# Moving the gate's blocks among key, value and query blocks, and the band values beside the heads' outputs, in a one-core encoder block

## The chip, the core and the metric

The kernel runs on one core of a Trainium2 chip. A core has five engines that run side by side, each in its own order: TensorE (PE, the matrix multiplier, with PEld its weight loads), VectorE (DVE), ScalarE (ACT), GpSimd (POOL) and SyncE (SP, which issues the DMAs here). Data lies in DRAM, in SBUF (128 partitions) and, for matmul results, in PSUM (eight banks of 128 partitions x 512 float32 values). The metric is the time of one execution in microseconds (us); lower is better.

## What is computed

One layer of an encoder on 512 tokens of width 1024: two token mixers on one normalised input, merged by gates, then cross-attention and a feed-forward part.

```python
h = rmsnorm(x, norm_mix[l])
qa, ka, va, za, alpha, beta, qb, kb, vb, ga, gb = _split_cols(h @ w_in[l], IN_SPLITS)
qkv = jax.nn.silu(_causal_dwconv(jnp.concatenate([qa, ka, va], axis=-1), conv_w[l]))
qa, ka, va = _split_cols(qkv, (A_QK, A_QK, A_VW))
oa = _gated_deltanet(qa, ka, va, alpha, beta, a_log[l], dt_bias[l])     # mixer A, 8 heads of 128
oa = rmsnorm(oa, head_norm[l]) * jax.nn.silu(za.reshape(b, s, A_HEADS, A_DV))
ob = _chunk_band_attention(qb, kb, vb, band_bias)                       # mixer B, 16 heads of 64
y = jax.nn.sigmoid(ga) * (oa @ w_a_out[l]) + jax.nn.sigmoid(gb) * (ob @ w_b_out[l])
x = x + y @ w_o[l]
x = x + _memory_xattn(rmsnorm(x, norm_xattn[l]), rmsnorm(mem, norm_mem[l]), ...)
x = x + (jax.nn.silu(gate) * up) @ w_down[l]
```

The gated delta rule of mixer A needs, for each head and each pair of chunks, the inverse of a unit lower triangular matrix I + L, where L comes from the keys' products k k^T. The value blocks, the gates and the band values depend on h alone.

## The kernel before

**Split matmuls.** Each weight tile is loaded (`raw`), copied to a reduced float form on ScalarE (`whi`, L114), and the rest, `raw - whi`, is formed as `wlo` (L116) on VectorE or GpSimd, whichever `lo_eng` names. The input h has a high and a low part too (`hh`, `hl`). A product is three matmuls: hi x hi, hi x lo, lo x hi (L140 to L142). A block (`block_steps`) is a projection to 128 features for all 512 tokens: eight steps of three matmuls of 512 columns. A natural group (`natural`, L165 to L167) has the tokens on the partitions: per 128 tokens eight steps of three matmuls of 256 columns. Tiles of raw, whi and wlo have three buffers each, of 128 x 1024 values.

**The stretch with keys and values.** Key blocks `k0` to `k7` (`ka` in PSUM) are followed by value blocks `v0` to `v7` (`va`), query blocks (`qa`) and, among them, groups `z1` to `z3` of mixer A's output gate za. A block's second part is put on a pending list and goes on one step at a time while later blocks issue their matmuls: for a key the causal convolution (`conv`, a ScalarE and three VectorE passes, L349 and L351), then `kT` (L355), twelve steps later four matmuls `kk` of the key with itself (L388), and the decay terms that give L (L412, L416 to L418; GpSimd's `PT` L401). For a value it is the convolution, `vT`, and twelve steps later four transposes `vn` (L499) and `vs` (L502).

**The inverse.** The diagonal 32 x 32 blocks of all L go to DRAM (`d1`) and come back as one tile `Lg`; `inverse_blocks` inverts them by 31 steps of two VectorE instructions on a growing tile: `sub` (L518) and `X` (L520). A copy (L523) and a way through DRAM (`d2`; writes, GpSimd's memsets L531, eight loads of X and eight of L, L539 and L540) follow, and then `inverse_levels` puts the blocks together on PE (first matmul `t`, L556), in four sets, two for each half of the loads, each a step apart.

**Behind it.** The queries go on, beside `states`, which runs the recurrence over the chunks. Then stands the gate of mixer A, `gate_a` (blocks `ga`, then ScalarE's tanh L655 into `sga`), beside `head_out` for each head: matmuls `oU` (L464) and `oS` (L468), ScalarE and VectorE work on the head's output, and its product with the za part (`zs`, L489). Then come the band values `vb_all` (natural groups, evacuated by ScalarE at L638), beside `oa_tiles`: per head four transposes `oaT` (L794) and the split `oah` (ScalarE) and `oal` (VectorE, L118); then `proj_a`, the projection of mixer A, and mixer B.

**What sets the order.** PE's order is the order in which the code emits its matmuls (`manual_schedule`). `drive` emits a main list of steps (blocks), after each advances what is pending, and adds `rate` steps of a side generator for each main step once `delay` steps have gone. The other engines' orders are set by a scheduler when the program is built; at run time each engine keeps its order and waits where an operand is missing. PSUM tags are `mm` (three buffers, blocks and natural groups), `ms` (two: kk, vn, kq, oU, oS, oaT) and `sd` (three, states and inverse levels).

```python
go("z1 k0 k1 k2 k3 k4 k5")
lo_eng[0] = nc.gpsimd
go("k6 k7")
go("v0 v1 v2 v3 v4 v5 z2 v6 v7 z3 q0 q1 q2", side=inverse_blocks(), rate=0.8, delay=22)
go("q3 q4 q5 q6 q7", side=states(), rate=1.0, delay=0)
lo_eng[0] = nc.vector
drive((gate_a(), None), side=seq(*[head_out(hd) for hd in heads]), rate=1.0, delay=12)
drive((vb_all(), None), side=oa_tiles(), delay=12, rate=0.2)
run_all(proj_a())
```

So `wlo` of k6, k7, all values, z2, z3 and all queries is GpSimd's work.

## Time and profile before

| | us |
|---|---|
| median of three runs | 1258.32 (1258.08 to 1258.97) |
| the profiled execution | 1259.04, its span 1257.3 |
| PE busy | 1222.9 (97%) |
| VectorE busy | 682.7 (54%) |
| ScalarE busy | 528.9 (42%) |
| GpSimd busy | 204.1 (16%) |

The page divides the span into 40 slices; a digit is the busy share in tenths, 9 for 90% or more. PE shows 9 in nearly all slices from the sixth on; VectorE shows 8 and 9 in the third to the sixth and 3 to 6 in most later ones. Starts in the rows are counted from the start of the span, and a row in a timeline gives start, duration, engine, line, operation, output and inputs, and in brackets the idle time before it with what ended it. The duration of a matmul is longer than its distance to the next, since matmuls are pipelined.

### The profile page before, as it was taken

The numbers are of one execution on the slowest core, as the hardware profiler recorded it, in microseconds if no ns is written. First come the engines' busy times: TensorE is split into PE (matmuls) and PEld (weight loads), VectorE is DVE, ScalarE is ACT, GpSimd is POOL, SyncE is SP. The second block draws the span as 40 slices with busy tenths as digits, with TensorE's granted clock in tenths as the row PEclk, the third lists the DMA queues.
The fourth block names the chain that finished last, engine by engine and source line by source line (L and its number), as shares of the span: only waits on it lengthen the run. The fifth ranks groups of instructions, "written<-read, shape, count | busy, mean of one in ns | idle before, by whom it ended". The sixth has DMA issues, their size and how long they took to land.

```text
span 1257.3 us, 17665 instructions
## 1 busy us (share of the span) xinstructions
PE 1222.9 (97%) x6899; PEld 1030.1 (82%) x6899; DVE 682.7 (54%) x1272; ACT 528.9 (42%) x1042; POOL 204.1 (16%) x158
## 2 busy tenths in 40 slices
PE   8998889999999999999999999999999999999997
PEld 7776787988898887777788898888888888888887
DVE  6989983564433378876355565446343443432234
ACT  6534235556442266765423444334332232222232
POOL 4356233201200000000122300003211111110000
PEclk9999989999999999999999999999999999999999
DMA  6253233122223333232334453213323323223343
GB/s 205 69 138 97 68 114 89 36 68 76 83 68 103 98 101 101 77 87 90 101 97 118 129 173 116 64 34 118 98 86 101 94 91 101 86 90 93 106 114 124
DMA packets 54612, 122.67 MB, mean 98 GB/s; under 512 B 16993, under 2 KB 23553, under 8 KB 54529
## 3 DMA queue, kind: packets, MB, share of 16 engines
q1 hardware_dynamic: 53440, 120.50, 31.9%
q8 instruction: 54, 0.88, 0.3%
q10 hardware_dynamic: 1088, 1.05, 0.2%
q14 instruction: 30, 0.24, 0.1%
HBM read 117.85 MB, written 3.69 MB: 97 GB/s over the span
## 4 chain that ended last, share of the span: by engine, by line
PE 84%; DVE 9%; issue 3%; ACT 2%; DMA 2%; POOL 1%; SPq 0%; POOLq 0%; DVEq 0%; ACTq 0%
PE ff L142 7%; PE ff L140 7%; PE ff L141 7%; PE g L140 5%; PE g L142 5%; PE g L141 5%; PE nat L165 2%; PE nat L167 2%; PE nat L166 2%; DVE conv L351 2%; PE pt L758 2%; PE ob L766 2%; PE qa L140 1%; DVE X L520 1%; PE kb L140 1%
## 5 line engine op out<-in xcount | busy, mean ns | idle before, releaser
L114 ACT ACTIVATE whi<-raw 128x1024 fp32r<-128x1024 f32 (+3 forms) x205 | 211.9, 1034 | 428.8 <-PE ff L141 157.7
L116 DVE TENSOR_TENSOR wlo<-raw,whi 128x1024 fp32r<-128x1024 f32 (+2 forms) x183 | 230.2, 1258 | 151.3 <-ACT whi L114 148.4
L140 PE MATMUL ff<-xh,whi 128*128 128x512 f32 x352 | 139.1, 395 | 0.0
L142 PE MATMUL ff<-xh,wlo 128*128 128x512 f32 x352 | 138.9, 395 | 0.0
L141 PE MATMUL ff<-xl,whi 128*128 128x512 f32 x352 | 138.9, 395 | 0.0
L206 POOL TENSOR_TENSOR acc<-acc,sq 128x512 f32<-128x512 f32 (+1 forms) x33 | 47.7, 1446 | 312.3 <-ACT sq L205 180.6
L142 PEld LDWEIGHTS ff<-xh,wlo 128*128 128x128 f32 x352 | 66.3, 188 | 15.5
L141 PEld LDWEIGHTS ff<-xl,whi 128*128 128x128 f32 x352 | 66.3, 188 | 15.5
L140 PEld LDWEIGHTS ff<-xh,whi 128*128 128x128 f32 x352 | 66.3, 188 | 15.3
L1058 POOL TENSOR_TENSOR fa<-fa,rrow 128x512 f32<-128x512 f32 x22 | 38.7, 1758 | 199.3 <-ACT fa L1057 194.1
L116 POOL TENSOR_TENSOR wlo<-raw,whi 128x1024 fp32r<-128x1024 f32 x22 | 53.2, 2420 | 85.9 <-ACT whi L114 76.3
L165 PE MATMUL nat<-whi,hh 128*128 128x256 f32 x192 | 57.7, 301 | 6.9 <-DVE conv L351 6.9
L1061 DVE TENSOR_TENSOR fb<-ff,fa 128x512 f32<-128x512 f32 x22 | 15.2, 692 | 77.1 <-PE ff L142 74.4
L166 PE MATMUL nat<-whi,hl 128*128 128x256 f32 x192 | 56.4, 294 | 0.0
L167 PE MATMUL nat<-wlo,hh 128*128 128x256 f32 x192 | 56.4, 294 | 0.0
L142 PE MATMUL g<-guh,wlo 128*128 128x512 f32 x132 | 51.4, 390 | 0.0
L141 PE MATMUL g<-gul,whi 128*128 128x512 f32 x132 | 51.4, 390 | 0.0
L140 PE MATMUL g<-guh,whi 128*128 128x512 f32 x132 | 51.4, 390 | 0.0
L1056 DVE TENSOR_TENSOR fa<-ff,rrow 128x512 f32<-128x512 f32 x22 | 15.2, 692 | 60.9 <-PE ff L142 59.4
L742 ACT ACTIVATE P<-P,mx 128x128 f32<-128x128 f32 (+1 forms) x64 | 35.8, 560 | 29.6 <-DVE mx L740 29.4
L728 POOL MEMSET bias<- 64x64 f32 x16 | 2.3, 144 | 265.5 <-DMA bias<-in_bias 248.3
L165 PEld LDWEIGHTS nat<-whi,hh 128*128 128x128 f32 x192 | 39.0, 203 | 7.7 <-issue 7.6
(380 smaller groups left out, 3189.0 us busy)
## 6 DMA issues: line engine op xcount, KB each, us to landing
raw<-in_w_g SPq DMA_DIRECT2D x22, 512.0 KB, 3.5
raw<-in_w_u SPq DMA_DIRECT2D x22, 512.0 KB, 3.5
raw<-in_w_d SPq DMA_DIRECT2D x20, 512.0 KB, 3.6
raw<-in_wk SPq DMA_DIRECT2D x8, 512.0 KB, 3.6
raw<-in_wv SPq DMA_DIRECT2D x8, 512.0 KB, 3.7
raw<-in_wq SPq DMA_DIRECT2D x8, 512.0 KB, 3.6
raw<-in_wga SPq DMA_DIRECT2D x8, 512.0 KB, 3.6
bias<-in_bias SPq DMA_DIRECT2D x16, 256.0 KB, 2.8
```

Of the source, the lines that this page charges most:

```text
L114: nc.scalar.activation(hi, src, AF.Copy, scale=1.0 if scale is None else scale)
L116: (eng or nc.vector).tensor_tensor(out=lo, in0=src, in1=hi.bitcast(F32), op=ALU.subtract)
L140: nc.tensor.matmul(out=ps[:, :w], lhsT=hi[:, k - a, :], rhs=xh[:, n], start=first, stop=False)
L141: nc.tensor.matmul(out=ps[:, :w], lhsT=hi[:, k - a, :], rhs=xl[:, n], start=False, stop=False)
L142: nc.tensor.matmul(out=ps[:, :w], lhsT=lo[:, k - a, :], rhs=xh[:, n], start=False, stop=last)
L165: nc.tensor.matmul(out=o, lhsT=xh[:, tok], rhs=hi[:, kw, :], start=(k == 0), stop=False)
L166: nc.tensor.matmul(out=o, lhsT=xl[:, tok], rhs=hi[:, kw, :], start=False, stop=False)
L167: nc.tensor.matmul(out=o, lhsT=xh[:, tok], rhs=lo[:, kw, :], start=False, stop=(k == KD - 1))
L206: nc.gpsimd.tensor_tensor(out=acc, in0=acc, in1=sq, op=ALU.add)
L351: nc.vector.scalar_tensor_tensor(out=c[:, s:], in0=ps[:, : T - s], scalar=w(3 - s), in1=c[:, s:], op0=ALU.mult, op1=ALU.add)
L742: nc.scalar.activation(pr, pr, AF.Exp, scale=-1.0, bias=mx, accum_out=rs[:, t : t + 1])
L1058: nc.gpsimd.tensor_tensor(out=a, in0=a, in1=row3, op=ALU.mult)
```

## The change

**Gate blocks.** The eight blocks of `gate_a` are no longer a phase of their own. They are entries `g0` to `g7` of the lists that `go` works off, between key, value and query blocks; their `wlo` goes to GpSimd. After such a block `gate_after` applies the tanh into a temporary tile and writes it to DRAM (`dga`); `head_out` loads it back into `sga` for its head.

**Low parts.** `lo_eng` now stays on VectorE until q3. So the `wlo` of k6, k7, v0 to v7 and q0 to q2 moves from GpSimd to VectorE; the gate blocks, z2 and z3 (by the new argument `eng`) have theirs on GpSimd, and q3 to q7 as before.

**Band values and transposes.** `vb_all` stands beside the heads' outputs in place of the gate, with rate 1.5 and delay 6 where rate 1.0 and delay 12 stood. It evacuates through a temporary tile to DRAM (`dvb`), from where the eight `vb` tiles are loaded after `proj_a`. The transposes of a head and their split (`oa_tile`) become the last steps of the next head's `head_out`, with `oah` and `oal` in the tags `c` and `b`.

```diff
-    def weights(src, kt, width):
+    def weights(src, kt, width, eng=None):
...
-        split(hi, lo, raw, eng=lo_eng[0])
+        split(hi, lo, raw, eng=eng or lo_eng[0])
...
-    def gemm(store, name, w, hd):
+    def gemm(store, name, w, hd, eng=None):
         store[hd] = PM(name)
-        yield from block_steps(store[hd], w[hd], h)
+        yield from block_steps(store[hd], w[hd], h, eng=eng)
...
+        s = sga[hd] = G("b", "sga")
+        nc.sync.dma_start(out=s, in_=dga[hd])
+        if hd:
+            yield from oa_tile(hd - 1)
+        if hd == AH - 1:
+            yield from wait(6)
+            yield from oa_tile(hd)
+
+    sga, oa = {}, []
+
+    def oa_tile(hd):
+        z = zs[hd // 2]
+        o = (hd % 2) * P
+        pt = PS("oaT")
+        for n in range(NT):
+            nc.tensor.transpose(out=pt[:, n * P : n * P + P], in_=z[:, n, o : o + P], identity=ident)
+        hi, lo = G("c", "oah", F32R), G("b", "oal", F32R)
+        split(hi, lo, pt, gain(C_HN, 0))
+        oa.append((hi, lo))
+        yield
...
     def vb_all():
-        vb.extend([G("b", "vb") for _ in range(2)] for tt in range(NT))
         for g in range(4):
             def ev(tt, ps, g=g):
-                nc.scalar.activation(vb[tt][g // 2][:, (g % 2) * 256 : (g % 2) * 256 + 256], ps[:, 0:256], AF.Copy)
+                v = TMP("vbt", "c")[:, :256]
+                nc.scalar.activation(v, ps[:, 0:256], AF.Copy)
+                nc.sync.dma_start(out=dvb[tt, :, g * 256 : g * 256 + 256], in_=v)
             yield from natural(wvb[g], 256, h, NT, ev)
 
     def z_group(g):
-        yield from natural(wz[g - 1], 256, xg if g <= 1 else h, NT, z_evac(g))
+        yield from natural(wz[g - 1], 256, xg if g <= 1 else h, NT, z_evac(g), nc.gpsimd if g > 1 else None)
...
-    def gate_a():
-        for j in range(KD):
-            ps = PM("ga")
-            yield from block_steps(ps, wga[j], h)
-            s = G("b", "sga")
-            nc.scalar.activation(s, ps, AF.Tanh, scale=0.5)
-            sga.append(s)
-            yield
...
+    def gate_after(j):
+        s = TMP("sga", "th")
+        nc.scalar.activation(s, gaps[j], AF.Tanh, scale=0.5)
+        nc.sync.dma_start(out=dga[j], in_=s)
+        yield
...
+    gh = lambda j: (gemm(gaps, "ga", wga, j, nc.gpsimd), gate_after(j))
...
-    go("z1 k0 k1 k2 k3 k4 k5")
-    lo_eng[0] = nc.gpsimd
-    go("k6 k7")
+    go("z1 k0 k1 k2 k3 g0 k4 k5 g1 k6 k7 g2")
...
-    go("v0 v1 v2 v3 v4 v5 z2 v6 v7 z3 q0 q1 q2", side=inverse_blocks(), rate=0.8, delay=22)
+    go("v0 v1 g3 v2 v3 g4 v4 v5 g5 z2 v6 v7 g6 z3 q0 q1 g7 q2", side=inverse_blocks(), rate=0.8, delay=22)
...
-    drive((gate_a(), None), side=seq(*[head_out(hd) for hd in heads]), rate=1.0, delay=12)
+    drive((vb_all(), None), side=seq(*[head_out(hd) for hd in heads]), rate=1.5, delay=6)
...
-    drive((vb_all(), None), side=oa_tiles(), delay=12, rate=0.2)
     run_all(proj_a())
+    for tt in range(NT):
+        vb.append([G("b", "vb") for _ in range(2)])
+        for x in range(2):
+            nc.sync.dma_start(out=vb[tt][x], in_=dvb[tt, :, x * T : x * T + T])
```

**How instructions move.** The rows below are an engine's instructions in their order, with line, operation, output, inputs and shape; a number at a name's end only tells one tile from another.

PE, where the first inverse-level matmuls `t` stand. Before, v7, z3 and the whole of q0 (`qa_1991`) lie ahead of them, and q1 (`qa_2042`) goes on between the sets:

```order
L140 MATMUL qa_1991<-hh_548,whi_1994 128x512
L141 MATMUL qa_1991<-hl_549,whi_1994 128x512
L142 MATMUL qa_1991<-hh_548,wlo_1995 128x512
L556 MATMUL t_418_2022<-X_380_1767,L 32x32 x16
L140 MATMUL qa_2042<-hh_436,whi_2045 128x512
L141 MATMUL qa_2042<-hl_437,whi_2045 128x512
L142 MATMUL qa_2042<-hh_436,wlo_2046 128x512
L556 MATMUL t_427_2061<-X_380_1767,L 32x32 x16
```

After, v7 (`va_2002`) is the last block ahead of them, and g6 (`ga_2062`) goes on between the sets:

```order
L140 MATMUL va_2002<-hh_550,whi_2005 128x512
L141 MATMUL va_2002<-hl_551,whi_2005 128x512
L142 MATMUL va_2002<-hh_550,wlo_2006 128x512
L576 MATMUL t_419_2042<-X_385_1799,L 32x32 x16
L140 MATMUL ga_2062<-hh_438,whi_2065 128x512
L141 MATMUL ga_2062<-hl_439,whi_2065 128x512
L142 MATMUL ga_2062<-hh_438,wlo_2066 128x512
L576 MATMUL t_428_2081<-X_385_1799,L 32x32 x16
```

So z3 and q0 moved from ahead of the levels to behind them, and g0 to g5 now lie ahead.

VectorE in the inverse, at the same steps (`sub` and `X` of 24 x 8 to 21 x 11). Before, only the passes of `conv` and a `vs` stand between the steps:

```order
L520 TENSOR_TENSOR X_1349<-X_1349,sub_1420 128x24x8
L518 TENSOR_TENSOR sub_1445<-Lg_1347,X_1349 128x207
L520 TENSOR_TENSOR X_1349<-X_1349,sub_1445 128x23x9
L351 SCALAR_TENSOR_TENSOR conv_1499<-va_1423,cst,conv_1499 128x511
L518 TENSOR_TENSOR sub_1451<-Lg_1347,X_1349 128x220
L351 SCALAR_TENSOR_TENSOR conv_1499<-va_1423,cst,conv_1499 128x510
L520 TENSOR_TENSOR X_1349<-X_1349,sub_1451 128x22x10
L351 SCALAR_TENSOR_TENSOR conv_1499<-va_1423,cst,conv_1499 128x509
L502 TENSOR_TENSOR vs_1533<-vn_1528,dinv_970 128x512
```

After, a low part `wlo` stands there too:

```order
L540 TENSOR_TENSOR X_1453<-X_1453,sub_1518 128x24x8
L538 TENSOR_TENSOR sub_1543<-Lg_1451,X_1453 128x207
L540 TENSOR_TENSOR X_1453<-X_1453,sub_1543 128x23x9
L116 TENSOR_TENSOR wlo_1648<-raw_1645,whi_1647 128x1024
L538 TENSOR_TENSOR sub_1549<-Lg_1451,X_1453 128x220
L351 SCALAR_TENSOR_TENSOR conv_1532<-va_1459,cst,conv_1532 128x511
L540 TENSOR_TENSOR X_1453<-X_1453,sub_1549 128x22x10
L351 SCALAR_TENSOR_TENSOR conv_1532<-va_1459,cst,conv_1532 128x510
L538 TENSOR_TENSOR sub_1555<-Lg_1451,X_1453 128x231
L351 SCALAR_TENSOR_TENSOR conv_1532<-va_1459,cst,conv_1532 128x509
L540 TENSOR_TENSOR X_1453<-X_1453,sub_1555 128x21x11
```

So a weight's low part, GpSimd's before, moved in between two steps, with its convolution passes after it.

GpSimd from the memsets of X, just ahead of the inverse. Before, low parts of values, of z2 and z3 and of q0 follow (two tiles for a z group):

```order
L512 MEMSET X_1349 128x1024
L513 MEMSET X_1349 128x32
L116 TENSOR_TENSOR wlo_1492<-raw_1489,whi_1491 128x1024
L116 TENSOR_TENSOR wlo_1556<-raw_1553,whi_1555 128x1024
L116 TENSOR_TENSOR wlo_1562<-raw_1559,whi_1561 128x1024
L116 TENSOR_TENSOR wlo_1747<-raw_1744,whi_1746 128x1024
L116 TENSOR_TENSOR wlo_1784<-raw_1781,whi_1783 128x1024
L116 TENSOR_TENSOR wlo_1839<-raw_1836,whi_1838 128x1024
L116 TENSOR_TENSOR wlo_1845<-raw_1842,whi_1844 128x1024
L116 TENSOR_TENSOR wlo_1995<-raw_1992,whi_1994 128x1024
```

After, the low parts of g4, g5 and z2 (two) are left ahead of the memsets for the inverse's second half, with that of g6 behind them:

```order
L532 MEMSET X_1453 128x1024
L533 MEMSET X_1453 128x32
L116 TENSOR_TENSOR wlo_1583<-raw_1580,whi_1582 128x1024
L116 TENSOR_TENSOR wlo_1764<-raw_1761,whi_1763 128x1024
L116 TENSOR_TENSOR wlo_1816<-raw_1813,whi_1815 128x1024
L116 TENSOR_TENSOR wlo_1822<-raw_1819,whi_1821 128x1024
L551 MEMSET X_385_1799 128x1024
L551 MEMSET X_386_1801 128x1024
L116 TENSOR_TENSOR wlo_2066<-raw_2063,whi_2065 128x1024
```

So four low parts stand between the two pairs of memsets.

PE in the heads. Before, a head's `oU` and `oS` stand a step of a gate block (`ga`) apart:

```order
L464 MATMUL oU_3333<-vs_1533,PT_963 128x128 x4
L140 MATMUL ga_3298<-hh_509,whi_3301 128x512
L141 MATMUL ga_3298<-hl_510,whi_3301 128x512
L142 MATMUL ga_3298<-hh_509,wlo_3302 128x512
L468 MATMUL oS_3334<-L,qT_2579 128x128 x3
L140 MATMUL ga_3298<-hh_520,whi_3301 128x512
L141 MATMUL ga_3298<-hl_521,whi_3301 128x512
L142 MATMUL ga_3298<-hh_520,wlo_3302 128x512
```

After, the transposes `oaT` of the head before stand right ahead of a head's `oU`, and `oS` follows two steps of a natural group (`nat`) later:

```order
L506 MATMUL oaT_3664<-ident,zs_309 128x128 x4
L464 MATMUL oU_3674<-vs_1686,PT_959 128x128 x4
L165 MATMUL nat_3683<-whi_3607,hh_438 128x256
L166 MATMUL nat_3683<-whi_3607,hl_439 128x256
L167 MATMUL nat_3683<-wlo_3608,hh_438 128x256
L165 MATMUL nat_3683<-whi_3607,hh_472 128x256
L166 MATMUL nat_3683<-whi_3607,hl_473 128x256
L167 MATMUL nat_3683<-wlo_3608,hh_472 128x256
L468 MATMUL oS_3675<-L,qT_2837 128x128 x3
L165 MATMUL nat_3683<-whi_3607,hh_489 128x256
```

So the transposes moved from the phase behind the heads to a place among their matmuls, where `oaT` and `oS` are both tiles of the tag with two buffers.

## Rows read from the trace of the kernel before

**Rows 1.** The page, section 1: busy time, share of the span and instructions of each engine.

```profile
PE 1222.9 (97%) x6899; PEld 1030.1 (82%) x6899; DVE 682.7 (54%) x1272; ACT 528.9 (42%) x1042; POOL 204.1 (16%) x158
```

**Rows 2.** The view of windows: for each stretch its length, the busy time of each engine (with its instructions), the granted clock of PE, the busy share of the DMA engines and GB/s. The stretches are the whole of the key and value work looked at (k4's block to the first inverse-level matmuls), the inverse, and three heads beside the gate.

```profile
72.69:195.68 122.99, 106.60 (x566) 90.95 (x566) 106.09 (x242) 45.78 (x88) 60.83 (x34) 0.96 0.38 104
...
126.76:180.80 54.04, 46.01 (x263) 40.65 (x261) 52.17 (x93) 15.98 (x25) 17.58 (x8) 0.94 0.23 75
...
290.24:328.84 38.60, 38.60 (x227) 33.82 (x226) 18.18 (x46) 25.61 (x98) 6.14 (x7) 1.00 0.21 66
```

**Rows 3.** The view of waits of PE from 72 to 196 us: what the engine stood still for, in total, how often, and the longest.

```profile
PE kk L388 <- DVE kT L355: 7.0, 6, 1.4
PE nat L165 <- DVE conv L351: 6.9, 4, 3.2
PE vn L499 <- DVE vT L355: 3.5, 4, 1.7
```

**Rows 4.** The groups by line of PE in the window 72.69 to 195.68 us: count, busy time and mean of one, idle time before them. L141 and L142 have as many as L140; L166 and L167 as many as L165.

```profile
L140 PE MATMUL va<-hh,whi 128*128 128x512 f32 x64 | 25.5, 398 | 0.0
...
L165 PE MATMUL nat<-whi,hh 128*128 128x256 f32 x64 | 20.9, 326 | 6.9 <-DVE conv L351 6.9
...
L140 PE MATMUL ka<-hh,whi 128*128 128x512 f32 x26 | 10.5, 404 | 0.0
```

**Rows 5.** The timeline of PE: start, duration, instruction. The last kk group and what follows it; then, in a block of natural matmuls, the first and the last of thirteen that follow each other; then the second and the last matmul of 512 columns of q0's block, seventeen in a row.

```profile
111.85 1.16 PE L388 MATMUL kk<-kT 128*128 128x128 f32 x8 [1.43 <-DVE kT L355]
112.76 0.47 PE L140 MATMUL va<-hh,whi 128*128 128x512 f32 x1
...
157.54 0.28 PE L166 MATMUL nat<-whi,hl 128*128 128x256 f32 x1
...
158.97 0.28 PE L166 MATMUL nat<-whi,hl 128*128 128x256 f32 x1
...
191.74 0.39 PE L141 MATMUL qa<-hl,whi 128*128 128x512 f32 x1
...
195.36 0.39 PE L142 MATMUL qa<-hh,wlo 128*128 128x512 f32 x1
```

**Rows 6.** The groups by line of VectorE (DVE) in the inverse, 126.7 to 180.8 us.

```profile
L520 DVE TENSOR_TENSOR X<-X,sub 128x31 f32<-128x31 f32 (+15 forms) x31 | 18.9, 610 | 0.6
L518 DVE TENSOR_TENSOR sub<-Lg,X 128x31 f32<-128x31 f32 (+15 forms) x31 | 17.1, 550 | 1.2 <-DMA Lg<-d 0.7
L351 DVE SCALAR_TENSOR_TENSOR conv<-va,cst,conv 128x510 f32<-128x510 f32 (+2 forms) x16 | 11.9, 743 | 0.0
...
L502 DVE TENSOR_TENSOR vs<-vn,dinv 128x512 f32<-128x512 f32 x5 | 3.4, 683 | 0.0
L294 DVE SCALAR_TENSOR_TENSOR zs<-zt,zc 128x256 f32<-128x256 f32 x4 | 1.7, 420 | 0.7 <-ACT zt L293 0.7
```

**Rows 7.** Three timelines and two groups. The timelines of VectorE and of GpSimd (POOL) around 130.5 us; the view of the tile wlo from 72 to 181 us, its row for GpSimd (shortest, median and longest of one, first and last start); and from the page, section 5, VectorE's row for the same line over the whole span.

```profile
130.60 2.36 DVE L518 TENSOR_TENSOR sub<-Lg,X 128x112 f32<-128x112 f32 x1
132.99 0.28 DVE L520 TENSOR_TENSOR X<-X,sub 128x112 f32<-128x112 f32 x1
...
130.42 2.40 POOL L116 TENSOR_TENSOR wlo<-raw,whi 128x1024 fp32r<-128x1024 f32 x1 [3.25 <-ACT whi L114]
...
L116 POOL TENSOR_TENSOR wlo<-raw,whi x15: 2369/2399/2591, 73.5 to 176.3; 128x1024 fp32r<-128x1024 f32 x15
...
L116 DVE TENSOR_TENSOR wlo<-raw,whi 128x1024 fp32r<-128x1024 f32 (+2 forms) x183 | 230.2, 1258 | 151.3 <-ACT whi L114 148.4
```

**Rows 8.** The ends of the inverse. Timelines of VectorE (the first step and what it waited for; the copy behind the last step) and of SyncE's queue (SP: the load of L for the last block of the first half, and the last load); then the view of the tile X from 175 to 200 us, its row for the first inverse-level matmuls and its last line, how long DMAs on this tile took from issue to landing.

```profile
126.76 0.46 DVE L518 TENSOR_TENSOR sub<-Lg,X 128x31 f32<-128x31 f32 x1 [0.70 <-DMA Lg<-d]
...
179.73 1.06 DVE L523 COPY Lg<-X 128x1024 f32<-128x1024 f32 x1
...
187.58 0.49 SPq L540 DMA_DIRECT2D L<-d  x1
...
191.84 0.49 SPq L540 DMA_DIRECT2D L<-d  x1
...
L556 PE MATMUL t<-X,L x96: 191/191/212, 195.7 to 199.2; 32*32 32x32 f32 x96
...
DMA to landing us min/median/max: 2.3/2.7/4.4
```

**Rows 9.** The heads and what follows. From the page, section 5, ScalarE's (ACT) row for the high parts of weights; then groups by line of ScalarE and of VectorE from 338 to 388 us (band values and transposes), and of VectorE from 290.24 to 328.84 us (heads); then timelines of PE: an oU group and what follows it, and an oaT group and what follows it.

```profile
L114 ACT ACTIVATE whi<-raw 128x1024 fp32r<-128x1024 f32 (+3 forms) x205 | 211.9, 1034 | 428.8 <-PE ff L141 157.7
...
L114 ACT ACTIVATE oah<-oaT,cst 128x512 fp32r<-128x512 f32 x8 | 5.5, 686 | 7.4 <-PE oaT L794 7.4
...
L118 DVE SCALAR_TENSOR_TENSOR oal<-oaT,cst,oah 128x512 fp32r<-128x512 f32 x8 | 6.0, 749 | 15.6 <-ACT oah L114 15.6
...
L489 DVE SCALAR_TENSOR_TENSOR zs<-kT,f,zs 128x128 f32<-128x128 f32 x24 | 6.8, 348 | 6.9 <-POOL f L484 6.9
...
300.95 1.05 PE L464 MATMUL oU<-vs,PT 128*128 128x128 f32 x8
301.76 0.48 PE L140 MATMUL ga<-hh,whi 128*128 128x512 f32 x1
...
351.42 0.60 PE L794 MATMUL oaT<-ident,zs 128*128 128x128 f32 x4
351.78 0.36 PE L165 MATMUL nat<-whi,hh 128*128 128x256 f32 x1
```

More of the change, by code (lines that the diff above doesn't have):

```diff
@@ L125, in weights, with block_steps @@
         lo = wp.tile([P, kt, width], F32R, tag="wlo", bufs=3, name=nm("wlo"))
-        split(hi, lo, raw, eng=lo_eng[0])
+        split(hi, lo, raw, eng=eng or lo_eng[0])
         return hi, lo
     lo_eng = [nc.vector]
-    def block_steps(ps, src, act, kt=KD, pieces=None, n=slice(0, T)):
+    def block_steps(ps, src, act, kt=KD, pieces=None, n=slice(0, T), eng=None):
         pieces = pieces or [(0, kt)]
@@ L135, in block_steps @@
         for a, b in pieces:
-            hi, lo = weights(src[:, a:b, :] if (a, b) != (0, kt) else src, b - a, P)
+            hi, lo = weights(src[:, a:b, :] if (a, b) != (0, kt) else src, b - a, P, eng)
             for k in range(a, b):
@@ L147, in block, with natural @@
             pass
-    def natural(src, width, act, ntok, evac):
-        w = [weights(src[hf], 4, width) for hf in range(2)]
+    def natural(src, width, act, ntok, evac, eng=None):
+        w = [weights(src[hf], 4, width, eng) for hf in range(2)]
         for tt in range(ntok):
@@ L646, in seq @@
             yield from g
-    sga, chain = [], []
-    def gate_a():
-        for j in range(KD):
-            ps = PM("ga")
-            yield from block_steps(ps, wga[j], h)
-            s = G("b", "sga")
-            nc.scalar.activation(s, ps, AF.Tanh, scale=0.5)
-            sga.append(s)
-            yield
+    chain = []
+    dga = dp.tile([KD, P, T], F32, name="dga")
+    dvb = dp.tile([NT, P, D], F32, name="dvb")
+    gaps = {}
+    def gate_after(j):
[3 more added lines that the diff above has]
+        yield
     ap_ctx = tc.tile_pool(name="delta", bufs=1)
@@ L667, in hybrid_block @@
     qh = lambda hd: (gemm(qps, "qa", wq, hd), q_after(hd))
+    gh = lambda j: (gemm(gaps, "ga", wga, j, nc.gpsimd), gate_after(j))
     def go(spec, **kw):
-        drive(*[{"z": zg, "k": kh, "v": vh, "q": qh}[c](int(d)) for c, d in spec.split()], **kw)
-    go("z1 k0 k1 k2 k3 k4 k5")
-    lo_eng[0] = nc.gpsimd
-    go("k6 k7")
+        drive(*[{"z": zg, "k": kh, "v": vh, "q": qh, "g": gh}[c](int(d)) for c, d in spec.split()], **kw)
+    go("z1 k0 k1 k2 k3 g0 k4 k5 g1 k6 k7 g2")
     inner = tc.tile_pool(name="inverse", bufs=1)
     chain.append(inner.__enter__())
-    go("v0 v1 v2 v3 v4 v5 z2 v6 v7 z3 q0 q1 q2", side=inverse_blocks(), rate=0.8, delay=22)
+    go("v0 v1 g3 v2 v3 g4 v4 v5 g5 z2 v6 v7 g6 z3 q0 q1 g7 q2", side=inverse_blocks(), rate=0.8, delay=22)
     inner.__exit__(None, None, None)
@@ L784, in band_values @@
         ob.append((hi, lo))
-    oa = []
-    def oa_tiles():
-        for hd in range(AH):
-            z = zs[hd // 2]
-            o = (hd % 2) * P
-            pt = PS("oaT")
-            for n in range(NT):
-                nc.tensor.transpose(out=pt[:, n * P : n * P + P], in_=z[:, n, o : o + P], identity=ident)
-            hi, lo = V("oah", F32R), V("oal", F32R)
-            split(hi, lo, pt, gain(C_HN, 0))
-            oa.append((hi, lo))
-            yield
     ya = []
```

## The prediction

> **What bounds the kernel now.** I read the busy times first, then the waits of TensorE (PE), then windows, then the instructions of the two places that the change touches. PE is busy for 1222.9 of 1257.3 us [rows 1], so the end can only come earlier where PE stands still or runs slowly, and almost all of that lies ahead of 196 us. In the window from 72.69 us (k4's block) to 195.68 us (the first inverse-level matmuls) VectorE is busy 106 of 123 us [rows 2], and all that PE waits for there is VectorE's: 7.0 us for the key tiles, 6.9 us for a PSUM bank that the convolution still reads, 3.5 us for the value tiles [rows 3]. A busy PE is not a dense PE, so I count matmuls instead. Columns of 512 follow each other every 0.226 us (16 steps from 191.74 to 195.36), of 256 every 0.119 us (12 steps from 157.54 to 158.97), and a head's kk group takes 0.91 us (111.85 to 112.76) [rows 5]. The window holds (64 + 26) x 3 matmuls of 512 columns for v and k, 24 for q0's block, 192 of 256, six kk and eight vn groups (about 0.36 us each, as oaT's four transposes) [rows 3, 4, 9]: 66.4 + 22.8 + 5.5 + 2.9 = 97.6 us of dense work in 123.0. **25 us of PE are empty**, and that is what the change can win at most.
>
> **The gate's blocks.** Each is 24 x 0.226 = 5.4 us of PE, with no VectorE work of its own: its low part goes to GpSimd, its tanh to ScalarE (46 us busy in the window [rows 2]). Eight of them leave the stretch beside the heads, which was dense, and six go in between k3 and the inverse levels, the others right behind these. So far this is 25 us of empty time against 33 us to fill it. But the PE order is fixed, and a moved instruction waits where it stands. The inverse levels stood behind v7, z3 and q0; now they stand right behind v7, with g0 to g5 ahead of them. Ahead of them PE has 6 x 5.4 = 32.5 us more and 11.4 (z3: 96 x 0.119) + 5.4 (q0) = 16.8 us less, so 15.7 us more. If PE reached them at the same 195.68 us, the rest of the kernel would be shorter by **15.7 us**. What counts is when they can run.
>
> **When the levels can run: VectorE.** From the window's start, PE at dense pitch comes to the last kk group (k7's) after 168 x 0.226 + 5 x 0.91 = 42.5 us, at 115.2 us; before, it stood at 111.85 [rows 5]. The work in the key stage allows this: VectorE gets four or five low parts at 1.26 us [rows 7] and loses v0's convolution. From that kk group it was 14.9 us until the first inverse step got its data, at 126.76 [rows 8], so the inverse starts near 130 us, 3 us later. It lasted from 126.76 to 180.79: 54.0 us, VectorE 96% busy [rows 2, 8]. In the new order the same inverse steps and the same fifteen convolution passes lie in it, with three z products fewer (3 x 0.42 = 1.3), one v product more (0.7 [rows 6]) and three low parts more (3 x 1.26 = 3.8 [rows 7]).
>
> The term that decides is a collision. A low part on GpSimd takes 2.40 us, and the VectorE instruction that meets it is held as long: sub at 130.60 takes 2.36 us where its neighbour takes 0.28, under GpSimd's low part of 130.42 [rows 7]. Seven of the fifteen low parts on GpSimd fall into the inverse and all hit; the 36.0 us of its two lines [rows 6] hold seven such holds of 2.1 us, 14.7 us, which leaves 0.34 us a step, near that neighbour. In the new order GpSimd has four there (g4, g5, both halves of z2): 8.4 us, 6.3 less. Bounds: no hit, because a convolution pass, which the trace shows at an even 0.74 us, stands there instead (14.7 less), or seven as before (none less). I take four hits, nearest to the rows. So 54.0 - 1.3 + 0.7 + 3.8 - 6.3 = 50.9 us, and the inverse ends at 130 + 50.9 = 180.9, **where it ended before**.
>
> The Trainium skill (SBUF — State Buffer, section Who interferes with whom) states the same as a rule: a VectorE instruction with two SBUF inputs and a GpSimd instruction that reads SBUF exclude each other for a whole instruction. By it the low parts that move to VectorE, with two SBUF inputs, can be held or hold GpSimd as well, so one or two hits more (2 to 4 us) could come in the key stage; the sum above leaves that to its upper bound. Another of its rules (GPSIMD Engine Reference, Engine selection) speaks against this change: a two-input elementwise operation belongs on VectorE, since GpSimd takes about twice as long. The trace agrees, 2.40 against 1.26 us, and by it the gates would be cheaper with their low part on VectorE, at 1.26 instead of a hold of 2.1.
>
> From the inverse's end to the last load was 13.7 us (180.79; issue at 191.84, 2.7 to land), for the first half 9.5 us (187.58 + 2.7) [rows 8]. The sets of a level, between which pieces of blocks stand, spread over 3.5 us (195.7 to 199.2), and those of the second half alone need the last load, some 3 us in: so PE may start at 180.9 + 13.7 - 3 = 191.6. PE itself, dense, would be there at 72.69 + 97.6 + 15.7 = 186.0; but v1's and v2's transposes now stand before VectorE is done with them (4 and 2 us by estimate, since the inverse's first steps stand ahead of those convolutions and wait for the load). I take 193 us, 2.7 us earlier than before. **Gain up to here: 15.7 + 2.7 = 18.4 us.**
>
> **Behind the levels.** g6, z3, q0, q1, g7, q2 and the states keep their matmuls and pitch; the three queries' low parts go to VectorE, idle half the time by then. PE's clock was 0.94 of full in the inverse, halved after its stops [rows 2]; stops remain, and one half-rate stretch may now fall behind the levels: **1 us lost**.
>
> **Band values beside the heads.** vb's 384 matmuls, the heads' and the transposes only change places: PE was dense in both stretches (38.60 of 38.60 us in one [rows 2]). What is new is a bank. The heads' oS, the transposes oaT and q7's kq share one PSUM bank, oU has the other, and a head's oS follows the previous head's oaT after one oU (0.81 us [rows 9]) and six 256-column matmuls (0.72), 1.53 us. The bank is free after oah on ScalarE (0.69) and oal on VectorE (0.75), 1.44 us without hand-overs [rows 9]. With ScalarE 25.6 of 38.6 us busy [rows 2], and its load now that of shorter heads, I take 0.4 us of stop per head and 1 us at kq: 8 x 0.4 + 1, **4 us lost** (bounds: 0, and the rival below). The evacuations go to DRAM: 16 writes, 8 reads of dvb, 8 writes and 8 reads of dga on SyncE's queue, some 0.5 us an issue [rows 8]. Weight loads queued behind a write that waits for ScalarE have two blocks of slack (11 us); that hides them, and costs up to 3 us where it doesn't. The vb loads wait for the projection's last matmuls and hold the third band pair's weights up, needed 16 us later: nothing.
>
> **Sum.** 18.4 - 1 - 4 = 13.4 us, from the profiled execution's 1259.04 us (span 1257.3; 0.7 above the median of the runs): **1245.5 us**.
>
> **Rivals.**
> - VectorE stays the bound: no collision is saved and the added low parts come on top: inverse 54.0 - 1.3 + 0.7 + 3.8 = 57.2 us from 131, levels at 131 + 57.2 + 10.7 = 198.9. Gain 15.7 - 3.2 - 5 = 7.5, 1251. For it: VectorE was 96% busy; against it: GpSimd has fewer low parts there. 0.17.
> - PE becomes the bound: collisions miss (inverse 42 us), levels at 187, heads lose 2: gain 15.7 + 8.7 - 2 = 22, 1237. Against it: the v transposes. 0.10.
> - No change: SyncE's queue. A dga write that waits for its tanh stands ahead of weight or inverse loads; the levels at 206 (10.3 later) and 4 us lost behind them give 1259 - 15.7 + 10.3 + 4 = 1258. Decides from 12 us of delay; the slots allow 11. 0.08.
> - **Slower**: the shared bank. If whi (1.03), the low part (1.26) and the z products (4 x 0.35 = 1.39) stand ahead of oah and oal in their engines' order, a head's oS waits 1.03 + 0.69 + 1.26 + 1.39 + 0.75 - 1.53 = 3.6 us [rows 7, 9]; times seven heads is 25 us, and the time 1259 - 18.4 + 1 + 25 = 1267. It decides from 2.5 us per head. For it: both engines wait in order; against it: the order has 12 to 24 matmuls (1.4 to 2.9 us) ahead of most oaT. 0.09.
>
> **Chances.** Forecast 0.56, the others as given. A measurement tells this kernel's time from no change at about 0.2%, 2.5 us. Faster: 0.56 + 0.17 + 0.10 = 0.83; same 0.08; slower 0.09. The range for 8 in 10 reaches from just above PE-bound, 1237.5, to 1256, beyond the first rival with heads that lose 4 us more.
>
> **What the profile after would show.** Right: PE's waits ahead of the levels shrink from 17 us to under 10; the last inverse step ends within 3 us of 181; the levels start at 190 to 196 with g0 to g5 done; low parts on GpSimd in the inverse are four, each with one VectorE step over 2 us; oS waits for oal under 0.6 us a head. Wrong: levels after 199, a stop of over 2 us at each oS, or a weight load that ends a PE wait.

## The result, and the profile after

The changed kernel takes 1248.23 us (median of four runs, 1246.03 to 1248.71), the kernel before 1258.28 beside it: ratio 0.9916, 95% interval 0.9899 to 0.9933, so 10 us less. Two executions that ran far slower than all others (1498.57 us in experiment 2, 4138.17 us in experiment 8) are left out of the medians below. The profiled execution took 1248.53 us with a span of 1246.6, 10.5 us less than that of before.

The page's first section:

```profile
PE 1220.3 (98%) x6899; PEld 1029.2 (83%) x6899; DVE 687.6 (55%) x1277; ACT 528.2 (42%) x1042; POOL 190.6 (15%) x153
```

PE is busy 2.6 us less and the span is 10.7 us shorter [rows 1]: 8.1 us of the gain is time in which PE stood. The first waits of PE over the whole span (us in total, times, longest):

```profile
PE z L236 <- DVE xgl L118: 4.4, 3, 1.6
PE vn L519 <- DVE vT L355: 2.7, 3, 1.4
PE ka L142 <- DVE wlo L116: 2.6, 1, 2.6
PE kk L388 <- DVE edec L341: 1.4, 1, 1.4
PE kk L388 <- DVE kT L355: 1.3, 1, 1.3
PE psT L334 <- DVE Gs L331: 1.2, 1, 1.2
PE oS L468 <- DVE PT L454: 1.2, 1, 1.2
PE oaT L506 <- DVE zs L489: 1.2, 1, 1.2
...
```

Of the 17.4 us that PE stood ahead of the levels [rows 3], 4.0 are left (vn 2.7, kk 1.3). The waits for `edec`, for `PT` and for `zs` are new, and that for `Gs` was 0.4 us before; each turns up again below. The windows of the changed kernel (key stage, inverse, up to the levels, heads; columns as in [rows 2]):

```profile
72.00:132.10 60.10, 58.80 (x286) 49.28 (x285) 51.49 (x153) 28.36 (x55) 23.93 (x18) 1.00 0.44 125
132.10:182.20 50.10, 47.43 (x256) 40.14 (x255) 48.54 (x94) 16.12 (x25) 9.73 (x4) 1.00 0.31 102
182.20:195.08 12.88, 12.88 (x66) 10.71 (x65) 7.44 (x8) 5.11 (x8) 6.68 (x4) 1.00 0.76 161
315.60:358.70 43.10, 41.55 (x350) 40.61 (x349) 23.07 (x58) 29.45 (x114) 7.05 (x7) 1.00 0.40 119
```

VectorE (DVE) is busy in 48.5 of the inverse's 50.1 us, as it was in 52.2 of 54.0 before [rows 2]. The inverse is 3.9 us shorter, and PE has more work in it (47.4 us busy of 50.1, before 46.0 of 54.0) and keeps its full clock (1.00, where 0.94 stood). From the view of the tile X, the inverse-level matmuls (shortest, median and longest of one in ns, first and last start) and the landing times:

```profile
L576 PE MATMUL t<-X,L x128: 190/191/213, 195.1 to 200.4; 32*32 32x32 f32 x128
...
DMA to landing us min/median/max: 2.1/2.6/3.0
```

From SyncE's timeline the last load ahead of them:

```profile
192.60 0.49 SPq L560 DMA_DIRECT2D L<-d  x1
```

The levels start at 195.08 us, where they stood at 195.68 [rows 2, 8], with g0 to g5 done. PE did not wait for them: the last load landed at 195.2, and the sets that need it come some 3 us in, so the loads would have let PE start near 192.

**Where the 10.5 us come from.** 15.7 us of blocks moved ahead of a point that is reached 0.6 us earlier: 16.3 us. The 0.6 us are there already at the first key matmul (37.61 us, before 38.26), ahead of all that moved; counted from it, the levels come after 157.5 us, as before (157.4). From the levels to mixer B's first matmul the kernel before took 432.63 - 195.68 = 236.95 us and the changed one 421.99 - 195.08 = 226.91, 10.0 less, where 15.7 us of blocks are missing: 5.7 us were given back behind the levels.

The waits for `Gs` and `edec`, at 56 to 62 us, have a cause of their own. GpSimd (POOL) in the changed kernel, from its timeline (start, duration):

```profile
54.09 2.87 POOL L116 TENSOR_TENSOR wlo<-raw,whi 128x1024 fp32r<-128x1024 f32 x1 [11.84 <-ACT whi L114]
```

VectorE's timeline at the same time:

```profile
53.18 4.33 DVE L351 SCALAR_TENSOR_TENSOR conv<-kT,cst,conv 128x511 f32<-128x511 f32 x3
```

The second kk group on PE's timeline:

```profile
69.96 0.38 PE L388 MATMUL kk<-kT 128*128 128x128 f32 x2
```

And windows of 2 us between the two (the granted clock stands behind the busy times):

```profile
56.00:58.00 2.00, 1.05 (x5) 0.53 (x3) 2.00 (x2) 0.40 (x1) 0.96 (x1) 1.00 0.12 37
58.00:60.00 2.00, 0.99 (x4) 0.51 (x4) 1.94 (x7) 1.18 (x5) 0.00 (x0) 0.98 0.74 250
60.00:62.00 2.00, 1.35 (x6) 1.35 (x7) 1.28 (x3) 0.86 (x2) 0.00 (x0) 0.50 0.07 18
62.00:64.00 2.00, 2.00 (x8) 1.71 (x7) 1.86 (x11) 0.00 (x1) 0.23 (x1) 0.50 0.36 82
64.00:66.00 2.00, 2.00 (x7) 1.52 (x6) 0.12 (x2) 1.11 (x2) 0.79 (x1) 0.50 0.87 251
```

GpSimd's low part is that of g0. Under it the three convolution passes of the first key take 4.33 us; PE, which needs what VectorE makes next, is busy for 2.0 of the 4 us from 56 to 60, and then its granted clock is 0.50, the lower of its two levels (1.2 of 2.4 GHz), until about 67 us. The second kk group comes 32.4 us after the first key matmul (69.96 - 37.61), where it came 27.0 after it before (65.21 - 38.26).

### The profile page after: what moved, and what is told of

Its sections match the earlier page's. It is cut to its first block, busy times and chain, and to the rows that moved or that the text cites. A ratio compares the mean times of both kernels' runs of the same rounds, so it can differ in the third digit from the quotient of the medians.

```text
span 1246.6 us, 17768 instructions
## 1 busy us (share of the span) xinstructions
PE 1220.3 (98%) x6899; PEld 1029.2 (83%) x6899; DVE 687.6 (55%) x1277; ACT 528.2 (42%) x1042; POOL 190.6 (15%) x153
## 4 chain that ended last, share of the span: by engine, by line
PE 84%; DVE 7%; issue 3%; ACT 2%; DMA 2%; POOL 1%; SPq 0%; POOLq 0%; DVEq 0%; ACTq 0%
PE ff L140 7%; PE ff L141 7%; PE ff L142 7%; PE g L140 5%; PE g L142 5%; PE g L141 5%; PE nat L165 2%; PE nat L166 2%; PE nat L167 2%; PE pt L779 2%; PE ob L787 2%; DVE conv L351 1%; PE kb L140 1%; PE gb L140 1%; PE qb L140 1%
## 5 line engine op out<-in xcount | busy, mean ns | idle before, releaser
L116 DVE TENSOR_TENSOR wlo<-raw,whi 128x1024 fp32r<-128x1024 f32 (+2 forms) x188 | 236.2, 1257 | 144.7 <-ACT whi L114 141.9
L140 PE MATMUL ff<-xh,whi 128*128 128x512 f32 x352 | 139.1, 395 | 0.0
L142 PE MATMUL ff<-xh,wlo 128*128 128x512 f32 x352 | 138.9, 395 | 0.0
L141 PE MATMUL ff<-xl,whi 128*128 128x512 f32 x352 | 138.9, 395 | 0.0
L140 PEld LDWEIGHTS ff<-xh,whi 128*128 128x128 f32 x352 | 66.3, 188 | 15.5
L142 PEld LDWEIGHTS ff<-xh,wlo 128*128 128x128 f32 x352 | 66.3, 188 | 15.5
L141 PEld LDWEIGHTS ff<-xl,whi 128*128 128x128 f32 x352 | 66.3, 188 | 15.3
L116 POOL TENSOR_TENSOR wlo<-raw,whi 128x1024 fp32r<-128x1024 f32 x17 | 41.3, 2432 | 120.9 <-ACT whi L114 120.9
L165 PE MATMUL nat<-whi,hh 128*128 128x256 f32 x192 | 57.2, 298 | 0.0
L167 PE MATMUL nat<-wlo,hh 128*128 128x256 f32 x192 | 54.2, 282 | 0.1
L166 PE MATMUL nat<-whi,hl 128*128 128x256 f32 x192 | 54.2, 282 | 0.0
L142 PE MATMUL g<-guh,wlo 128*128 128x512 f32 x132 | 51.4, 390 | 0.0
L141 PE MATMUL g<-gul,whi 128*128 128x512 f32 x132 | 51.4, 390 | 0.0
L140 PE MATMUL g<-guh,whi 128*128 128x512 f32 x132 | 51.4, 390 | 0.0
L165 PEld LDWEIGHTS nat<-whi,hh 128*128 128x128 f32 x192 | 36.7, 191 | 0.8
L166 PEld LDWEIGHTS nat<-whi,hl 128*128 128x128 f32 x192 | 36.7, 191 | 0.1
```

The source lines that it names most:

```text
L116: (eng or nc.vector).tensor_tensor(out=lo, in0=src, in1=hi.bitcast(F32), op=ALU.subtract)
L140: nc.tensor.matmul(out=ps[:, :w], lhsT=hi[:, k - a, :], rhs=xh[:, n], start=first, stop=False)
L141: nc.tensor.matmul(out=ps[:, :w], lhsT=hi[:, k - a, :], rhs=xl[:, n], start=False, stop=False)
L142: nc.tensor.matmul(out=ps[:, :w], lhsT=lo[:, k - a, :], rhs=xh[:, n], start=False, stop=last)
L165: nc.tensor.matmul(out=o, lhsT=xh[:, tok], rhs=hi[:, kw, :], start=(k == 0), stop=False)
L166: nc.tensor.matmul(out=o, lhsT=xl[:, tok], rhs=hi[:, kw, :], start=False, stop=False)
```

## The experiments

Ten kernels ran, all timed in turn with the kernel before; times are medians. Where "levels" are given, it is the first `t` matmul. Experiments 5 and 7 leave everything ahead of the levels as it is in the changed kernel; counted from the first key matmul, their traces have the levels after 158.2 and 156.5 us, that of the changed kernel after 157.5. So a difference at the levels between two traces holds to about 1 us.

**1. g0's low part on VectorE.** In the changed kernel:

```diff
-    gh = lambda j: (gemm(gaps, "ga", wga, j, nc.gpsimd), gate_after(j))
+    gh = lambda j: (gemm(gaps, "ga", wga, j, nc.gpsimd if j else None), gate_after(j))
```

> The changed kernel with one edit: g0's low part on VectorE instead of GpSimd. Theory (in the changed kernel GpSimd's low part of g0 at 54.1 us holds the first key's convolution 2 us, PE then stops and its clock halves, 5 us lost): the three passes take 2.3 us again, the second kk group comes at 64.5 to 65.5 us instead of 69.96, no half-clock stretch at 60 to 66 us, the inverse starts and ends 4 to 5 us earlier, levels at 190 to 191.5: 1243 to 1245 us. Rival (VectorE is the bound there anyway, the 1.26 us that it gets costs as much as the hold): 1247.5 to 1249 us.

Measured: 1244.81 us, ratio 0.9893 (0.9880 to 0.9906), and levels at 191.43. The first key's convolution, from VectorE's timeline:

```profile
54.04 2.31 DVE L351 SCALAR_TENSOR_TENSOR conv<-kT,cst,conv 128x511 f32<-128x511 f32 x3
```

Windows of the same place as above:

```profile
60.00:62.00 2.00, 2.00 (x11) 1.65 (x10) 2.00 (x12) 1.06 (x3) 0.01 (x1) 1.00 0.41 162
62.00:64.00 2.00, 2.00 (x10) 1.67 (x9) 1.35 (x7) 1.32 (x2) 1.39 (x1) 1.00 0.20 47
```

The theory holds: 2.31 us in place of 4.33, the clock at full, the second kk group at 65.42, and the inverse still takes 50.2 us but starts 3.8 and ends 3.7 us earlier. Counted from the first key matmul, the levels come 152.8 us later, in the changed kernel 157.5: the one hold cost 4.7 us at the levels and 3.4 us of the time. VectorE had room for the 1.26 us.

**2. All low parts until q3 on VectorE.** In the changed kernel:

```diff
-    gh = lambda j: (gemm(gaps, "ga", wga, j, nc.gpsimd), gate_after(j))
+    gh = lambda j: (gemm(gaps, "ga", wga, j), gate_after(j))
...
-        yield from natural(..., z_evac(g), nc.gpsimd if g > 1 else None)
+        yield from natural(..., z_evac(g))
```

> The changed kernel with the low parts of all gate blocks and of z2 and z3 on VectorE; GpSimd has none until q3. Theory (a low part on GpSimd costs VectorE a hold of 2.1 us, more than the 1.26 us of doing it): no VectorE step over 2 us in the inverse, which lasts 50.1 - 4 x 2.1 + 4 x 1.26 = 46.8 us, and the early hold is gone as well: levels at 187 to 190, 1241 to 1244 us. Rival (GpSimd spares VectorE what it takes over): the inverse lasts 54 to 55 us, 1250 to 1253 us.

Measured: 1243.2 us (three runs, 1240.6 to 1243.5), ratio 0.9872 (0.9855 to 0.9889); levels at 190.51. The time lies in the theory's range, the levels half a microsecond behind theirs. The groups by line of VectorE in the inverse (count, busy time, mean ns of one, idle time before), of the changed kernel:

```profile
L540 DVE TENSOR_TENSOR X<-X,sub 128x31 f32<-128x31 f32 (+15 forms) x31 | 14.6, 472 | 0.5
L538 DVE TENSOR_TENSOR sub<-Lg,X 128x31 f32<-128x31 f32 (+15 forms) x31 | 12.7, 410 | 1.6 <-DMA Lg<-d 1.0
L351 DVE SCALAR_TENSOR_TENSOR conv<-va,cst,conv 128x511 f32<-128x511 f32 (+2 forms) x15 | 11.1, 741 | 0.0
L355 DVE SCALAR_TENSOR_TENSOR vT<-th,conv 128x512 f32<-128x512 f32 x5 | 5.2, 1049 | 0.3 <-ACT th L354 0.3
...
L116 DVE TENSOR_TENSOR wlo<-raw,whi 128x1024 fp32r<-128x1024 f32 x3 | 3.7, 1218 | 0.0
```

And of this one:

```profile
L540 DVE TENSOR_TENSOR X<-X,sub 128x31 f32<-128x31 f32 (+15 forms) x31 | 10.5, 338 | 0.6
L538 DVE TENSOR_TENSOR sub<-Lg,X 128x31 f32<-128x31 f32 (+15 forms) x31 | 10.5, 338 | 1.2 <-DMA Lg<-d 0.7
L116 DVE TENSOR_TENSOR wlo<-raw,whi 128x1024 fp32r<-128x1024 f32 x8 | 9.8, 1223 | 0.8 <-ACT whi L114 0.5
```

Without GpSimd's low parts the 62 steps take 21.0 us, 0.34 each; with four of them 27.3, and `vT` 1.8 more: 8.1 us for four holds. But eight low parts of 1.22 us lie in the inverse here, five more than in the changed kernel, and two of the za products that lay behind it there: so it lasts 48.5 us, not 46.8. Against experiment 1 the whole is 1.6 us faster, of which the trace shows 0.9 at the levels.

**3. The other low parts back on GpSimd.** In the changed kernel:

```diff
-    go("z1 k0 k1 k2 k3 g0 k4 k5 g1 k6 k7 g2")
+    go("z1 k0 k1 k2 k3 g0 k4 k5 g1")
+    lo_eng[0] = nc.gpsimd
+    go("k6 k7 g2")
```

> The changed kernel with the low parts of k6, k7, all values and q0 to q2 back on GpSimd, as before the change; the gate blocks stay where they are, on GpSimd too. So this is the gate's move and the heads' part without the move of the low parts. Theory (holds set the inverse): eight low parts on GpSimd in the inverse, each holds a step: 50.1 + 4 x 2.1 - 4 x 1.26 = 53 to 55 us, more holds ahead of it, levels at 199 to 202: 1252 to 1256 us. Rival (the gain is the filled PE alone, whoever makes the low parts): 1247 to 1250 us.

Measured: 1249.49 us, ratio 0.9933 (0.9921 to 0.9945), levels at 196.32. The theory falls on the time, which lies in the rival's range: the gate's move without that of the low parts keeps 8.8 of the 10 us. Seven steps were held in the inverse, and the two lines in [rows 6] have 36.0 us here as there, but the inverse lasts 51.9 us only: the changed kernel's three low parts are out of it, and all four za products, which lay in the inverse before, come behind its last step. PE waits longer for the value tiles, 6.2 us (2.7 in the changed kernel). Against that, after the same hold by g0's low part the clock stays at 1.00 in the profiled execution, the fastest of the five (1248.76 us). Two of its windows of 2 us:

```profile
58.00:60.00 2.00, 0.98 (x4) 0.51 (x4) 1.94 (x5) 1.57 (x5) 0.00 (x0) 1.00 0.65 240
60.00:62.00 2.00, 0.75 (x6) 0.75 (x7) 1.88 (x6) 0.26 (x2) 0.00 (x0) 1.00 0.03 8
```

The second kk group comes 29.6 us after the first key matmul (67.74 - 38.17), not 32.4. From that group to the levels it takes 128.6 us, 3.5 more than the changed kernel (125.1). So, by these two traces, the engine of the low parts is worth some 3.5 us in that stretch, and the halved clock ahead of it costs the changed kernel 2.8 us, which hides most of that.

**4. The move of the low parts alone.** In the kernel before:

```diff
-    lo_eng[0] = nc.gpsimd
     go("k6 k7")
...
-        yield from natural(wz[g - 1], 256, xg if g <= 1 else h, NT, z_evac(g))
+        yield from natural(wz[g - 1], 256, xg if g <= 1 else h, NT, z_evac(g), nc.gpsimd if g > 1 else None)
```

(with the argument `eng` in `weights` and `natural`.)

> The kernel before with the move of the low parts alone: those of k6, k7, the values and q0 to q2 on VectorE, z2 and z3 and later on GpSimd; gate, heads and band values as before. Theory (it takes the empty PE time and something to fill it with): the inverse is 54.0 + 3.8 - 3 x 2.1 = 51.5 us, with more VectorE work ahead of it: 1255 to 1258.5 us. Rival (the moved low parts are the gain): 1247 to 1251 us.

Measured: 1257.33 us, ratio 0.9991 (0.9982 to 1.0000). The time lies in the theory's range, but for another reason. PE reaches the levels at 189.46, 6.2 us earlier than before. The inverse takes 56.2 us (126.4 to 182.6), not 51.5, with four holds and 3.5 us in which VectorE stands for ScalarE's part of two za products; so now PE waits for the loads. From its waits, 186 to 220 us:

```profile
PE t L556 <- DMA X<-d: 2.0, 2, 1.6
```

From the view of the tile X, 180 to 225 us:

```profile
L556 PE MATMUL t<-X,L x128: 184/228/258, 189.5 to 198.4; 32*32 32x32 f32 x128
...
L575 PE MATMUL t<-X,L x64: 218/218/268, 209.7 to 217.4; 64*64 64x64 f32 x64
```

And windows of the stop, of what follows it and of the rest of the levels:

```profile
188.80:193.40 4.60, 2.56 (x69) 1.80 (x68) 2.25 (x3) 2.37 (x4) 2.36 (x1) 0.98 1.03 126
193.40:203.40 10.00, 10.00 (x144) 7.10 (x143) 1.51 (x3) 3.64 (x9) 0.00 (x0) 0.50 0.54 132
203.40:217.60 14.20, 14.20 (x292) 11.08 (x290) 6.65 (x16) 7.45 (x20) 2.38 (x1) 1.00 0.12 39
```

Behind the stop PE runs for 10 us at the lower of its two levels, by estimate 5 us lost at half the pace, and the last of these matmuls starts at 217.4; in the kernel before it starts at 217.8, with the clock at 1.00 from the first level matmul on. The single executions agree: eleven of the twelve have a mean granted clock of 0.986 to 0.990 and take 1256.01 to 1258.80 us; the twelfth has 0.993 and takes 1251.89 (where its clock stayed up was not seen). So the moved low parts alone do bring PE forward, and in most executions nearly all of that goes to the stop at the loads and to the clock behind it.

**5. The transposes in another bank.** In the changed kernel:

```diff
-        pt = PS("oaT")
+        pt = PD("oaT")
```

> The changed kernel with the transposes oaT in the PSUM tag with three buffers, which the states have left by then, so that a head's oS no longer waits for oah and oal. Theory (the bank costs little: one stop of 0.2 us for oal stands in the waits of the changed kernel, and three intervals of 0.33 to 0.48 us ahead of an oS): 0.3 to 0.9 us less, 1247.3 to 1248 us. Rival (the prediction's term, 0.4 us a head): 3.2 us less, 1245 us.

Measured: 1247.06 us (1244.27 to 1247.56), ratio 0.9901 (0.9888 to 0.9915); the runs overlap with those of the changed kernel, so the trace decides. There the stop for `oal` is gone, those for `PT` and `zs` (1.2 and 1.1 us) are not, and from the last level matmul to the projection it takes 159.5 us, 1 us less than in the changed kernel (160.5). This bank costs about 1 us, not 3.

**6. The heads' part alone.** In the kernel before, band values beside the heads (written to DRAM and loaded back as in the change, not shown here), gate beside the transposes:

```diff
-    drive((gate_a(), None), side=seq(*[head_out(hd) for hd in heads]), rate=1.0, delay=12)
+    drive((vb_all(), None), side=seq(*[head_out(hd) for hd in heads]), rate=1.0, delay=6)
...
-    drive((vb_all(), None), side=oa_tiles(), delay=12, rate=0.2)
+    drive((gate_a(), None), side=oa_tiles(), delay=12, rate=0.2)
```

> The kernel before with the heads' part alone: band values beside the heads at rate 1.0 and delay 6, kept in DRAM and loaded after the projection, and the gate's blocks, in one piece behind them, beside the transposes; key and value stretch as before. Theory (what this part costs in the changed kernel is two stops at its two ends, of which the one at the last head's transposes can't be here): 0 to 1.5 us more than before, 1258 to 1260 us. Rival (the shorter matmuls beside the heads leave ScalarE and VectorE too little time for each head): 3 to 5 us more, 1261 to 1263 us.

Measured: 1258.26 us, ratio 0.9997 (0.9988 to 1.0006), and no wait of PE at all from 200 to 440 us. Band values beside the heads and the way through DRAM (16 writes and 8 loads of `dvb`) cost nothing that can be measured; what the heads cost in the changed kernel is left to what is not here, rate 1.5 and the transposes among the heads.

**7. The two stops of the heads.** In the changed kernel:

```diff
-        pu_, pq = PS("oU"), PS("oS")
+        pu_, pq = PS("oU"), PD("oS")
...
-            yield from wait(6)
+            yield from wait(10)
             yield from oa_tile(hd)
```

> The changed kernel with oS in the PSUM tag with three buffers (so the second head's oS does not wait until PT of q7 has left its bank) and ten steps instead of six ahead of the last head's transposes. Theory (these two stops, 1.2 us each in the waits, 1.4 to 1.5 us of PE each, are most of what the heads' part costs): 2 to 3 us less, 1245 to 1246 us. Rival (the stops move: oU waits for PT, the projection for the last oal): 1247 to 1248.5 us.

Measured: 1243.86 us (1243.61 to 1244.02), ratio 0.9880 (0.9867 to 0.9894): 4.4 us less, more than expected. From the last level matmul to the projection it takes 156.2 us, 4.2 less than in the changed kernel. In the waits of the changed kernel from 315 to 380 us the three that this takes away:

```profile
PE oS L468 <- DVE PT L454: 1.2, 1, 1.2
PE oaT L506 <- DVE zs L489: 1.2, 1, 1.2
PE oS L468 <- DVE oal L118: 0.2, 1, 0.2
```

They show 2.6 us of the 4.2; the intervals between matmuls hold more, 1.49 us behind the last `kq` at 322.85, 1.48 ahead of the last transposes (from 364.59), and three of 0.33 to 0.48 ahead of an `oS`. With `oS` in the other tag it shares a bank neither with `kq` nor with the transposes.

**8 and 10. Both.** Experiments 2 and 7 together, run twice:

> The changed kernel with all low parts until q3 on VectorE, and with oS's other tag and ten steps ahead of the last transposes. Theory (the two gains lie in different stretches and add): 1240 to 1241.5 us. Rival (they do not add): 1243 us and more.

> e8_both again, whose profile fell into an execution in which everything ran some three times slower. Theory (both gains add): 1237 to 1240.5 us, levels at 190 to 191.5, and no stop over 1 us in the heads. Rival: 1243 us.

Measured: 1238.4 us (four runs, 1236.7 to 1239.8), ratio 0.9836 (0.9823 to 0.9850), and 1237.15 us (1236.82 to 1238.24), ratio 0.9838 (0.9824 to 0.9851); the profile is from the second. The gains add: 20 to 21 us less than before, 10 to 11 less than the changed kernel, where 5.0 and 4.4 were measured singly. The waits of PE from 37 to 440 us:

```profile
PE kk L388 <- DVE kT L355: 2.8, 2, 2.5
PE ka L142 <- DVE wlo L116: 2.6, 1, 2.6
PE psT L334 <- DVE Gs L331: 0.3, 1, 0.3
```

And the window of the heads, in which PE is busy throughout:

```profile
308.30:366.90 58.60, 58.60 (x500) 58.30 (x499) 28.86 (x69) 37.51 (x133) 10.11 (x12) 1.00 0.42 125
```

**9. Three gate blocks ahead of the levels.** In the changed kernel:

```diff
-    go("v0 v1 g3 v2 v3 g4 v4 v5 g5 z2 v6 v7 g6 z3 q0 q1 g7 q2", ...)
+    go("v0 v1 v2 v3 v4 v5 z2 v6 v7 z3 q0 q1 g3 g4 g5 g6 g7 q2", ...)
```

> The changed kernel with only g0 to g2 ahead of the inverse levels, in the key stage; g3 to g7 stand behind q1, and z3 and q0 are ahead of the levels again, as before the change. PE has 3 x 5.5 = 16.5 us more ahead of the levels than before, as much as in the changed kernel (15.7), but all of it in the key stage. Theory (empty PE time is won only in the stretch where a block stands): the inverse has the stops of the kernel before back, starts at 131 to 133 us and ends at 186 to 189, levels at 199 to 202: 1251 to 1254 us. Rival (it only counts how much lies ahead of the levels): levels at 195 to 196, 1247 to 1249 us.

Measured: 1250.92 us, ratio 0.9948 (0.9934 to 0.9962). The inverse lasts from 132.1 to 188.9 and the levels start at 199.38, as the theory has it; the time lies just under its range. It is 2.7 us behind the changed kernel with as much work ahead of the levels: VectorE has four za products in the inverse (one in the changed kernel) and more convolution passes (21 against 15), and PE has stops again (1.8 us for a bank behind `sub`, 0.5 for one behind `conv`). A gate block is the better filling there; that it is so because it brings VectorE nothing fits these counts and was not tested by itself.

## Why the prediction was right, and where it was off

1245.5 us was forecast, 1248.23 measured: right way, inside the range, and 10 us of the 13.4. In the sum's two parts, 18.4 us ahead of the levels measured 16.3, and 5 us lost behind them measured 5.7. (The sum's terms give 1245.6.)

- **The filled stops, 15.7 us: right.** Experiment 3 keeps 8.8 of the 10 us with this part and the heads' part alone, 6 shows that the heads' part alone brings nothing, 4 that the low parts alone bring 0.9 us in the median, though 6.4 in the one execution with the higher mean clock. What is new with 3 is that the move of the low parts counts for only 1.3 us of the changed kernel's time.
- **The inverse, 50.9 us: right, 50.1.** Four low parts on GpSimd, each with one VectorE instruction held: 8.1 us against 8.4 in the sum. One of the four was not a step but `vT`. No low part in the inverse met a convolution pass, so the bound "no hit" did not come true.
- **"The work in the key stage allows this": the step that failed.** It counted low parts by their duration, put further hits aside as an upper bound, and began its count at the kk group of 72.69 us as if nothing ahead of that moved. But g0's low part is made at 54.09, and there VectorE had no slack: it held the first key's convolution, and with the clock that fell behind PE's stop that cost 4.7 us at the levels (experiment 1). The kk group of 72.69 us came at 76.31 (in experiment 1 at 72.19), and the inverse began at 132.1, not at 130 (in experiment 1 at 128.3).
- **The levels at 193 us: they came at 195.08.** The inverse ended at 182.2, the loads would have done for 192, and PE came last, as it does in experiment 1 (191.43, where the loads would have done for 188.4). Its stops for the value transposes were 2.7 us, where 6 stood in the estimate. The term was 2.7 us and measured 0.6, which is no more than the earlier start; in experiment 1 it is 4.3 (195.68 - 191.43), 4.6 counted from the first key matmul. So without g0's hold the term would have been too small.
- **The clock, 1 us behind the levels: wrong place.** It stayed at full from 72 us through the inverse and to the end of the heads; it fell at 60 us, ahead of all that. Of the 4.7 us some 2.8 are the clock's, by the comparison with experiment 3.
- **The heads, 4 us: right in sum by luck, wrong in shares.** 4.2 us measured by experiment 7. The sum had 0.4 us a head for the bank of oS and oaT and 1 for `kq`. The bank with oaT is about 1 us in all (experiment 5); a stop of some 1.4 us at `kq` was there; one of 1.4 at the last head's transposes, six steps behind a chain that takes longer, was not in the sum.
- **SyncE's queue: no stop.** The only waits of PE for a DMA up to the levels are in experiment 4, for the inverse's own loads. The rival of the shared bank named a mechanism that is there, at 1 us where it had 25.

What stays open: why the clock fell after the hold in the changed kernel, and in the traces of experiments 5, 7 and 9 too, and not in experiment 3, where PE stood about as long. What the clock costs differs between executions of one kernel as well: of the changed kernel's four, three have a mean granted clock of 0.994 and take 1247.93 to 1248.71 us, the fourth has 0.996 and takes 1246.03. Of the 5.7 us behind the levels, experiment 7 leaves 1.5, of which 0.8 lie between the first and the last level matmul (22.9 us against 22.1). In experiment 10 it takes 221.7 us from the levels to mixer B (410.45 - 188.73), which leaves 0.5; which of its edits took the rest away was not tested.
